# SwiGLU's first product by one level of Strassen's algorithm, in a hybrid gMLP and gated-linear-attention layer

## The chip, the cores and the metric

The kernel runs on one NeuronCore of a Trainium2 chip. A core has five engines with an instruction queue of their own: TensorE (PE; matmuls into PSUM, weights loaded by PEld), VectorE (DVE), ScalarE (ACT), GpSimd (POOL) and SyncE (SP), which here only issues DMAs. The metric is device microseconds of one launch; the fewer the better. A profiled execution gives the trace from which all rows are read.

## The reference

One layer of a diffusion trunk on 512 latent tokens of width 2048 with 256 context tokens. After the mixer comes the part that is changed:

```
x   = x + mod[2] * rms_norm(y @ w_out, g_post_mix)
h   = modulate(rms_norm(x, g_pre_ffn), mod[3], mod[4])      # 512 x 2048
a,b = split(h @ w_ffn_in, 2)                                # 2048 x 11264: a and b are 512 x 5632
f   = (silu(a) * b) @ w_ffn_out                             # 5632 x 2048
out = x + mod[5] * rms_norm(f, g_post_ffn)
mod = split(silu(c) @ w_mod + b_mod, 6)                     # w_mod 2048 x 12288
```

All inputs are float32.

## The kernel before

Every large product is made of float32r matmuls. An operand is split into two parts, a high one (a cast on ACT) and the rest (a subtraction on DVE), and `three` (L291) adds three products of the parts into one PSUM bank: high x high, high x low, low x high. So each weight tile of 128 rows and 512 columns costs one cast and one subtraction of 512 columns, and three matmuls for each stationary block of 128.

`stream` (L278) walks over the row tiles of a weight matrix: two row tiles per DMA of 512 KB on SP's queue, a split for each (four buffers for either part), then the caller's matmuls, then `pump` (L274), which emits some steps of background work: `bg` and `bgm` are lists of generators with a rate of steps per row tile. One of them is `mod_row` (L250): it sums 16 row tiles of w_mod times a per-partition scalar on DVE (L225, 1024 columns each, three load buffers, one accumulator), and adds up the partitions by a product with ones that is pinned in PE's order (`keep_in_program_order`). All other instructions are ordered by the planner of the framework: it takes, engine by engine, the first instruction in code order that is ready by its own model of durations, and the order so found is fixed in the program.

The stages that matter here, in order:

* Output projection (`project`, L984): four column blocks of w_out (tiles wo); the last is done for tokens 0 to 255 and 256 to 511 one after the other. Beside it run the modulation rows m20 and m21 (the gate of the mixer). `residual` (L994) and `make_h2` (L1013) of the first half of tokens run beside the last block's second half; `make_h2` transposes the normalised tokens on PE (tiles h2p), modulates on ACT and splits into h2h and h2l.
* SwiGLU: 11 groups of 512 hidden units. `ffn_in` (L1052) makes a and then b of a group, hidden-major: 16 row tiles x 4 blocks of 128 hidden units x 3 matmuls of 512 tokens (tiles f). The first group's a is done over the first 256 tokens and then over the others, since h2 of those comes later. `hidden` (L1062) applies SiLU, multiplies and splits (gh, gl). Every two groups (`chunks`) the second product follows (tiles fo): four column blocks x 8 row tiles x 4 token tiles x 3, added up in SBUF (facc). The modulation rows m50 and m51 run beside the chunks from the second on.
* The end: the last group's second product (fz), token tile by token tile, with norm, gate and residual behind each.

SBUF is shared out by hand: 44 slots of 512 columns (`slot`), 33 in a second pool (`fslot`), the stream's pool `stg`. PSUM has six banks for accumulation and two for all else (`bank`).

Of the kernel before, what the change touches and what calls it, by code (L numbers as in the profile page):

```python
# [18 lines left out]
P = 128  # L19
D = 2048  # L20
# [12 lines left out]
NF = 33  # L33
# [17 lines left out]
class Pump:  # L51
    """Background work, emitted in small steps between the steps of the weight streams; lanes take turns"""
# [39 lines left out]
def trunk_kernel(ctx, tc, cmat, cmask, x, c, ctxt, c_ctx, w_mod, b_mod, g_pre_mix, g_post_mix, g_pre_ffn,  # L92
# [7 lines left out]
    stg = ctx.enter_context(tc.tile_pool(name="stg", bufs=1))  # L100
# [13 lines left out]
    # ---- constants and small vectors  # L114
# [21 lines left out]
    def rstd(ss, n, scale, name, eng=None):  # L136
        """1 / sqrt(scale ss + eps): a first guess from the exponent's bits, then Newton steps"""
# [19 lines left out]
    def rstd_exp(ss, n, name):  # L157
        """the same for tokens' sums over four column blocks, from ScalarE's logarithm and exponential and a Newton step"""
# [24 lines left out]
    # ---- adaLN: w_mod columns in blocks, rows accumulated on VectorE, summed over partitions on TensorE  # L183
# [48 lines left out]
    def mod_ab(base, k0, nk, cvec, gv, A, B, name, tiles, pin=False, late=0):  # L232
        """shift and scale of nk channel tiles -> per-channel scalars A = g (1 + scale), B = shift"""
# [16 lines left out]
    def mod_row(base, cb, grow, dst, name):  # L250
        """1024 columns of a gate as rows (every partition), times the post-norm gain"""
        n = f"{name}{cb}"
        for acc in mod_acc(base + cb * 1024, 1024, 1, cx, n, mod_bg):
# [3 lines left out]
        for j in range(2):  # L257
# [5 lines left out]
            V.tensor_tensor(out=dst[b], in0=ps, in1=gb, op=ALU.mult)  # L263
            yield

    # ---- weights: streamed, split into two float32r parts
# [11 lines left out]
    def stream(w, c0, ncol, nk, name, k_first=0):  # L278
        """(k, [(hi, lo) per 512 columns]) for the 128-row tiles of w"""
# [11 lines left out]
    def three(o, a, b, start, stop, lhs_first=True):  # L291
        """o += a^T b from the parts of both; a is the stationary operand"""
# [7 lines left out]
    # ---- x: root mean square, transpose  # L300
# [6 lines left out]
    def squares(tok, ss, j):  # L307
        """a token tile's sums of squares"""
# [25 lines left out]
    def turn(o, tok, k, diag=None):  # L334
        """channel tile k, channel-major"""
# [22 lines left out]
    def gate_weights(name):  # L358
        """the 32 columns of w_in for the low-rank gates, all rows: both parts beside each other, per channel tile"""
# [11 lines left out]
    def low_rank(o, w, h, start, stop):  # L371
        """the gates' low-rank products: rows 0-31 with the high part of the weights, rows 32-63 with the low part"""
# [5 lines left out]
    def modulated(k):  # L378
        """channel tile k of x, normalised and modulated, in two float32r parts"""
# [17 lines left out]
    # ---- first products of x as the modulation arrives, in two halves of the channels: d, k and the last head of q;  # L397
    # the other heads of q
# [5 lines left out]
    def land(ps, dst, first, scale=1.0, rows=P):  # L404
        """a part of a sum over channels, or a further part onto it"""
# [5 lines left out]
    def mod_both(k0):  # L411
        """shift and scale of two channel tiles for x and for the context: products on TensorE, which waits for them"""
# [114 lines left out]
    # ---- context: normalised and transposed, modulated by its own adaLN  # L527
# [52 lines left out]
    # ---- spatial gating  # L580
# [65 lines left out]
    # ---- context: d, k, v  # L646
# [32 lines left out]
    # ---- gated linear attention  # L679
# [23 lines left out]
    def log_decay(dsrc, h, p, name):  # L703
        """log-sigmoid of the gates of head h, tokens of two chunks: [token, (chunk, direction, key)]"""
# [11 lines left out]
    def keyed(b, dr_, nch, kT, dst):  # L716
        """k exp(b_last - b)"""
# [52 lines left out]
    def gla_scores(h):  # L770
# [16 lines left out]
        # scores inside a chunk, both directions: S^T[j, i]  # L787
# [11 lines left out]
        def weigh(s):  # L799
            """k and q times the decays to the boundary of their half of a block of 2 s tokens"""  # L800
# [43 lines left out]
    def gla_states(h):  # L844
# [9 lines left out]
        # states  # L854
# [27 lines left out]
        # outputs, channel-major, over the head's k and q  # L882
# [32 lines left out]
    # ---- values of the attention, token-major  # L915
# [13 lines left out]
    # ---- output gate of the attention, and both halves split for the output projection  # L929
# [35 lines left out]
    # ---- output projection, residual, norm before the FFN  # L965
    fp = ctx.enter_context(tc.tile_pool(name="fp", bufs=1))
# [3 lines left out]

    gate = [slot(f"gm{b}") for b in range(4)]
# [9 lines left out]
    h2h = [None] * KT  # L981
    h2l = [None] * KT

    def project(cg, toks, name):  # L984
        accs = [bank(f"{name}{t}") for t in toks]
        for k, (wp,) in stream(w_out[0], cg * 512, 512, KT, name):
# [7 lines left out]
    def residual(t0):  # L994
        """of two token tiles: x1 = x + gate * norm(y), kept in DRAM; then x1 over its root mean square"""
# [17 lines left out]
    def make_h2(half):  # L1013
        o = half * 256
        for k0 in range(0, KT, 2):
            ps = bank(f"h2p{half}_{k0}", False)
            tmp = slot(f"h2f{half}_{k0}")
            for j in range(2):
                k = k0 + j
                c = slice(j * 256, (j + 1) * 256)  # L1020
                turn(ps[:, c], yo[half * 2:half * 2 + 2], k)
                S.activation(tmp[:, c], ps[:, c], AF.Identity, bias=fmodB[:, k:k + 1], scale=fmodA[:, k:k + 1])
                if half == 0:
                    h2h[k] = fslot(f"h2h{k}", F32R)
                    h2l[k] = slot(f"h2l{k}", F32R)
                V.tensor_copy(h2h[k][:, o:o + 256], tmp[:, c])
                V.tensor_tensor(out=h2l[k][:, o:o + 256], in0=tmp[:, c], in1=h2h[k][:, o:o + 256].bitcast(F32),
                                op=ALU.subtract)
# [7 lines left out]
    for half in range(2):  # L1036
# [4 lines left out]
        bg.add(make_h2(half))  # L1041

    # ---- SwiGLU, hidden units in chunks, the second product summed over chunks
    gate2 = [None] * 4

    def mods_ffn():
        for b in range(4):
            gate2[b] = slot(f"gf{b}")
        for b in range(2):
            yield from mod_row(5 * D, b, g_post_ffn, gate2, "m5")  # L1050

    def ffn_in(gi, part, cols=((0, 512),)):  # L1052
        accs = [bank(f"f{gi}{part}{b}") for b in range(4)]
        for c0, n in cols:
            if c0:
# [115 lines left out]
```

## Time and profile before

| | us |
|---|---|
| median of 3 runs | 2407.95 |
| lowest, highest | 2407.12, 2409.24 |
| span of the profiled execution | 2405.3 |
| PE, DVE, ACT busy in it | 2349.8, 1221.4, 863.7 |

The span runs from the first to the last instruction of the profiled execution; a launch's time holds in addition what lies before and behind, and the median of the runs is 2.65 us above the span. Busy time of PE is modelled from each matmul's start, and matmuls overlap in the pipeline, so the distance between starts tells the pace, not the duration.

### The profile page before, as it was taken

To read this page: it belongs to the slowest core of one execution; us is meant where nothing else is said; L and a number is where in the kernel's file an instruction comes from. 1 tells how busy PE (TensorE), PEld (TensorE's weight loads), DVE (VectorE), ACT (ScalarE), POOL (GpSimd) and SP (SyncE) were. 2 spreads that over 40 slices of the span, in tenths; PEclk is the share of its full clock that TensorE was granted. 3 is DMA by queue.
4 is the path that set the end of the run, shared out by engine and by line. 5 is a ranking of instruction groups with operands and counts; after the bars stand their busy time and mean duration, and the time that the engine had idled before them with its cause. 6 is when DMAs were issued, how large, how long until landed. Compare 5 with 4: busy or idle time off the path is not lost.

```text
span 2405.3 us, 28755 instructions
## 1 busy us (share of the span) xinstructions
PE 2349.8 (98%) x10930; PEld 1932.2 (80%) x10930; DVE 1221.4 (51%) x1958; ACT 863.7 (36%) x1595; POOL 15.3 (1%) x22
## 2 busy tenths in 40 slices
PE   7999998999999999999999999999999999999998
PEld 2778887788887787888888888888888888888886
DVE  3876587677878747533234344333323332323347
ACT  4453344554564237523332222232222322323223
POOL 0000000000000000000000000000000000000000
PEclk9999999999999999999999999999999999999999
DMA  9967788644446847533244444433333323333335
GB/s 333 330 195 261 252 280 269 205 140 132 132 148 211 300 160 224 166 96 97 97 149 140 140 132 149 140 121 99 97 97 97 96 97 97 97 97 97 97 104 184
DMA packets 197507, 381.91 MB, mean 159 GB/s; under 512 B 17349, under 2 KB 28829, under 8 KB 197369
## 3 DMA queue, kind: packets, MB, share of 16 engines
q1 hardware_dynamic: 192992, 373.88, 48.0%
q10 hardware_dynamic: 4376, 6.20, 0.8%
q8 instruction: 85, 1.39, 0.2%
q14 instruction: 54, 0.43, 0.1%
HBM read 367.44 MB, written 12.58 MB: 158 GB/s over the span
## 4 chain that ended last, share of the span: by engine, by line
PE 89%; DMA 4%; DVE 4%; ACT 2%; issue 1%; SPq 0%; ACTq 0%; DVEq 0%
PE f L112 40%; PE fo L112 17%; PE wo L112 6%; PE vv1a L112 2%; PE g0a L112 2%; PE v0a L112 2%; PE u1a L112 2%; PE cv L112 2%; PE k L112 2%; PE vv0a L112 2%; PE v1a L112 2%; PE q L112 1%; PE g1a L112 1%; PE u L112 1%; PE s L112 1%; PE o L112 1%
## 5 line engine op out<-in xcount | busy, mean ns | idle before, releaser
L112 PE MATMUL f<-h2h,f_0h 128*128 128x512 f32 (+1 forms) x1472 | 561.1, 381 | 5.3 <-ACT f_0h L270 5.3
L271 DVE TENSOR_TENSOR f_0l<-f_r,f_0h 128x512 fp32r<-128x512 f32 x368 | 253.8, 691 | 610.5 <-ACT f_0h L270 577.8
L112 PE MATMUL f<-h2l,f_0h 128*128 128x512 f32 (+1 forms) x1472 | 560.0, 381 | 0.0
L112 PE MATMUL f<-h2h,f_0l 128*128 128x512 f32 (+1 forms) x1472 | 559.4, 381 | 0.0
L270 ACT CAST f_0h<-f_r 128x512 fp32r<-128x512 f32 x368 | 229.1, 623 | 657.3 <-PE f L112 616.3
L112 PEld LDWEIGHTS f<-h2h,f_0h 128*128 128x128 f32 x1472 | 277.5, 189 | 58.5 <-ACT f_0h L270 5.5
L112 PEld LDWEIGHTS f<-h2l,f_0h 128*128 128x128 f32 x1472 | 277.5, 189 | 52.5 <-issue 0.5
L112 PEld LDWEIGHTS f<-h2h,f_0l 128*128 128x128 f32 x1472 | 276.9, 188 | 52.6 <-DVE f_0l L271 0.2
L112 PE MATMUL fo<-fo_0h,gh 128*128 128x512 f32 x640 | 249.8, 390 | 0.0
L112 PE MATMUL fo<-fo_0h,gl 128*128 128x512 f32 x640 | 249.0, 389 | 0.0
L112 PE MATMUL fo<-fo_0l,gh 128*128 128x512 f32 x640 | 249.0, 389 | 0.0
L271 DVE TENSOR_TENSOR fo_0l<-fo_r,fo_0h 128x512 fp32r<-128x512 f32 x160 | 110.5, 691 | 263.7 <-ACT fo_0h L270 253.6
L270 ACT CAST fo_0h<-fo_r 128x512 fp32r<-128x512 f32 x160 | 99.8, 624 | 306.6 <-PE fo L112 267.9
L112 PEld LDWEIGHTS fo<-fo_0l,gh 128*128 128x128 f32 x640 | 120.1, 188 | 25.4 <-DVE fc L1108 0.2
L112 PEld LDWEIGHTS fo<-fo_0h,gh 128*128 128x128 f32 x640 | 120.1, 188 | 25.4 <-issue 0.5
L112 PEld LDWEIGHTS fo<-fo_0h,gl 128*128 128x128 f32 x640 | 120.1, 188 | 24.8
L112 PE MATMUL wo<-wo_0l,yh 128*128 128x512 f32 x256 | 101.3, 396 | 2.1 <-DVE wo_0l L271 2.1
L112 PE MATMUL wo<-wo_0h,yh 128*128 128x512 f32 x256 | 102.0, 402 | 0.0
L112 PE MATMUL wo<-wo_0h,yl 128*128 128x512 f32 x256 | 101.6, 397 | 0.0
L112 PEld LDWEIGHTS wo<-wo_0l,yh 128*128 128x128 f32 x256 | 48.9, 191 | 13.5 <-DVE wo_0l L271 2.6
L112 PEld LDWEIGHTS wo<-wo_0h,yh 128*128 128x128 f32 x256 | 48.6, 190 | 10.8 <-issue 0.5
L112 PEld LDWEIGHTS wo<-wo_0h,yl 128*128 128x128 f32 x256 | 48.9, 191 | 10.2
(811 smaller groups left out, 3401.5 us busy)
## 6 DMA issues: line engine op xcount, KB each, us to landing
f_r<-in_w_ffn_in_dram SPq DMA_DIRECT2D x184, 512.0 KB
fo_r<-in_w_ffn_out_dram SPq DMA_DIRECT2D x80, 512.0 KB
mx4w<-in_w_mod_dram SPq DMA_DIRECT2D x16, 512.0 KB
mx8w<-in_w_mod_dram SPq DMA_DIRECT2D x16, 512.0 KB
mx12w<-in_w_mod_dram SPq DMA_DIRECT2D x16, 512.0 KB
mc4w<-in_w_mod_dram SPq DMA_DIRECT2D x16, 512.0 KB
mc8w<-in_w_mod_dram SPq DMA_DIRECT2D x16, 512.0 KB
mc12w<-in_w_mod_dram SPq DMA_DIRECT2D x16, 512.0 KB
```

What stands on the lines that cost most here:

```text
L112: return T.matmul(o, lhsT=l, rhs=r, start=start, stop=stop)
L270: S.copy(wh[:, :n], src)
L271: V.tensor_tensor(out=wl[:, :n], in0=src, in1=wh[:, :n].bitcast(F32), op=ALU.subtract)
```

## The change

The first product is one level of Strassen's algorithm in Winograd's form. h is cut in two halves of tokens (rows) and two of channels (columns): A11, A12 for tokens 0 to 255, A21, A22 for the others. A group's weights are cut in the two halves of channels and in the columns of a and of b: B11, B12, B21, B22. Seven products of 256 tokens x 1024 channels x 512 columns take the place of eight:

```
S1=A11 S2=A12 S4=A22 S5=A22-A21 S6=S5+A11 S7=A21-A11 S3=A12-S6     (once, in make_top and make_rest)
T1=B11 T2=B21 T5=B11+B12 T6=T5+B22 T4=T6+B21 T3=B22 T7=B12+B22     (per group, on DVE, in float32)
a of tokens 0-255 = P1+P2; the other three quarters from P1, P3 to P7 by sums of results
```

(the signs are those of the kernel's weight sums.) The S operands are split once and stay in SBUF (56 tiles); they are the stationary operand now and the weights move, so the results come token-major: each product has two PSUM banks, one per token tile. Of the weights, B11 to B22 are loaded 28 times 512 KB per group where it was 16, and each of the seven T is split by one cast and one subtraction of 1024 columns. After the results' sums, SiLU and product, 16 transposes per group turn the activations hidden-major, and they go to DRAM (`g_dr`). The second product starts when all groups are done, reads them back (`hidden`), splits them and runs in two chunks of 20 row tiles; the last four row tiles are the end, as before, with their weights loaded and split during the last column block.

Other parts: the pool `stg` is closed after the attention and a pool `st2` opened at the same side of SBUF, with four buffers X (the running T sum; loads and accumulators of the modulation rows too), four load buffers R, three of 1024 columns for either part. m50 and m51 are made beside the projection, behind m20 and m21, at a rate of 1.5 steps per row tile (1.2 before), and kept as rows in DRAM.

```diff
-NF = 33
+NF = 29
...
-    stg = ctx.enter_context(tc.tile_pool(name="stg", bufs=1))
+    stg_ctx = ExitStack()
+    stg = stg_ctx.enter_context(tc.tile_pool(name="stg", bufs=1, side="right"))
...
-    def mod_row(base, cb, grow, dst, name):
+    def mod_row(base, cb, grow, dst, name, tiles, keep=None):
...
+            o = gb if keep is not None else dst[b]
+            V.tensor_tensor(out=o, in0=ps, in1=gb, op=ALU.mult)
+            if keep is not None:
+                nc.scalar.dma_start(keep[b:b + 1, :], o[0:1, :])
...
+    stg_ctx.close()
+    fp = ctx.enter_context(tc.tile_pool(name="fp", bufs=1, reuse_waits="tile"))
+    st2 = ctx.enter_context(tc.tile_pool(name="st2", bufs=1, side="right", reuse_waits="tile"))
...
+    def parts(src, name):
...
+        wh = st2.tile([P, 1024], F32R, tag="wh", bufs=3, name=name + "h")
+        wl = st2.tile([P, 1024], F32R, tag="wl", bufs=3, name=name + "l")
+        S.copy(wh, src)
+        V.tensor_tensor(out=wl, in0=src, in1=wh.bitcast(F32), op=ALU.subtract)
+        return wh, wl
...
+    def stream2(w, c0, k_first, nk, name):
...
+        for k0 in range(0, nk, 2):
+            t = wide(w, (k_first + k0) * P, c0, raw2(f"{name}r{k0}"), name)
+            pair = parts(t, f"{name}{k0}")
+            for j in range(2):
+                yield k0 + j, cut(pair, j * 512, 512)
+                pump()
...
         for b in range(2):
-            yield from mod_row(2 * D, b, g_post_mix, gate, "m2")
+            yield from mod_row(2 * D, b, g_post_mix, gate, "m2", mod_late)
+        for b in range(2):
+            yield from mod_row(5 * D, b, g_post_ffn, None, "m5", mod_late, gate2_dr)
...
-    bgm.rate = 1.2
+    bgm.rate = 1.5
...
+    def make_top():
+        for i, p in ((0, 1), (1, 2)):
+            for q in range(NQ):
+                top[i][q] = h2_pair(0, i * KT // 2 + 2 * q)
+                s_parts(p, q, top[i][q], fslot)
+                yield
...
+    def make_rest():
+        for q in range(NQ):
+            a21 = h2_pair(1, 2 * q)
+            a22 = h2_pair(1, KT // 2 + 2 * q)
+            a11, a12 = top[0][q], top[1][q]
+            s_parts(4, q, a22, slot)
+            V.tensor_tensor(out=a22, in0=a22, in1=a21, op=ALU.subtract)
+            s_parts(5, q, a22, slot)
+            V.tensor_tensor(out=a22, in0=a22, in1=a11, op=ALU.add)
+            s_parts(6, q, a22, slot)
+            V.tensor_tensor(out=a21, in0=a21, in1=a11, op=ALU.subtract)
+            s_parts(7, q, a21, slot)
+            V.tensor_tensor(out=a12, in0=a12, in1=a22, op=ALU.subtract)
+            s_parts(3, q, a12, slot)
             yield
...
+    def product(p, q, accs, wp, nq):
+        hi, lo = SP[p][q]
+        for j in range(2):
+            for t in range(2):
+                c = slice(j * 256 + t * P, j * 256 + (t + 1) * P)
+                three(accs[t], (hi[:, c], lo[:, c]), cut(wp, j * 512, 512), q == 0 and j == 0, q == nq - 1 and j == 1)
...
+        ps = two(n + "p1")
+        for q in range(NQ):
+            X[q] = blk(0, 0, q, chain_tile(f"{n}X{q}"))
+            product(1, q, ps, parts(X[q], f"{n}a{q}"), NQ)
+            pump()
+        u = [fslot(f"{n}u{t}") for t in range(2)]
+        for t in range(2):
+            S.copy(u[t], ps[t])
+        ps = two(n + "p2")
...
+        if gi == 0:
+            bg.drain()
...
+        p5 = two(n + "p5")
+        for q in range(NQ):
+            r = blk(0, 1, q, raw2(f"{n}c{q}"))
+            V.tensor_tensor(out=X[q], in0=X[q], in1=r, op=ALU.add)
+            product(5, q, p5, parts(X[q], f"{n}c{q}"), NQ)
+        p6 = two(n + "p6")
...
+        vtt(u, u, p6, ALU.subtract)
+        u4 = [fslot(f"{n}w{t}") for t in range(2)]
+        vtt(u4, p5, u, ALU.add)
+        p4 = two(n + "p4")
...
+        vtt(u, p4, u, ALU.add)
...
+        p7, p3 = two(n + "p7"), two(n + "p3")
+        for q in range(NQ):
+            z = blk(1, 1, q, raw2(f"{n}z{q}"))
+            y = blk(0, 1, q, raw2(f"{n}y{q}"))
+            product(3, q, p3, parts(z, f"{n}z{q}"), NQ)
+            V.tensor_tensor(out=y, in0=y, in1=z, op=ALU.add)
+            product(7, q, p7, parts(y, f"{n}y{q}"), NQ)
+        vtt(u, u, p7, ALU.subtract)
+        for t in range(2):
+            S.activation(u[t], u[t], AF.Silu)
+        b2 = [fslot(f"{n}v{t}") for t in range(2)]
+        vtt(b2, p7, u4, ALU.subtract)
+        vtt(u4, p3, u4, ALU.subtract)
+        vtt(a1, a1, u4, ALU.mult)
+        vtt(u, u, b2, ALU.mult)
+        toks = a1 + u
+        for f in range(4):
+            ps = bank(f"{n}T{f}", False)
+            for t in range(NT):
+                T.transpose(ps[:, t * P:(t + 1) * P], toks[t][:, f * P:(f + 1) * P], ident)
+            gt = slot(f"{n}t{f}")
+            S.copy(gt, ps)
+            nc.scalar.dma_start(g_dr[gi * 4 + f], gt)
...
+    def hidden(k0, nk):
...
+        for k in range(k0, k0 + nk, 2):
+            r = raw2(f"gr{k}")
+            nc.sync.dma_start(r.rearrange("p (k c) -> p k c", k=2), g_dr[k:k + 2].rearrange("k p c -> p k c"))
...
+    for ci, (k1, nk) in enumerate(((0, 20), (20, 20))):
         gT = []
...
+            if ci and cg == 3:
+                bg.add(last_weights())
+                bg.rate = 0.5
```

(`vtt` does one DVE operation for each of two token tiles, `blk` loads a weight block of two row tiles, `two` takes two banks.)

## Rows read from the trace of the kernel before

**Rows 1.** The page: span, busy time per engine, GB/s per slice, costliest group.

```profile
span 2405.3 us, 28755 instructions
...
PE 2349.8 (98%) x10930; PEld 1932.2 (80%) x10930; DVE 1221.4 (51%) x1958; ACT 863.7 (36%) x1595; POOL 15.3 (1%) x22
...
GB/s 333 330 195 261 252 280 269 205 140 132 132 148 211 300 160 224 166 96 97 97 149 140 140 132 149 140 121 99 97 97 97 96 97 97 97 97 97 97 104 184
...
L112 PE MATMUL f<-h2h,f_0h 128*128 128x512 f32 (+1 forms) x1472 | 561.1, 381 | 5.3 <-ACT f_0h L270 5.3
...
```

**Rows 2.** Chain that ended last, SwiGLU: start us, length us, engine, tile, line, count.

```profile
...
979.36 151.26 PE f L112 x746
1130.62 87.04 PE fo L112 x384
1217.66 174.08 PE f L112 x768
...
```

**Rows 3.** Busy time by stretch, us; then TensorE clock, DMA share, GB/s.

```profile
...
802.00:842.00 40.00, 40.00 (x177) 32.83 (x176) 31.11 (x34) 7.80 (x13) 0.95 (x1) 1.00 0.88 303
...
940.70:979.40 38.70, 33.44 (x258) 32.48 (x258) 31.03 (x79) 29.02 (x66) 0.00 (x0) 0.91 0.68 212
...
2004.60:2265.70 261.10, 261.10 (x1153) 216.20 (x1152) 78.34 (x117) 71.73 (x118) 0.00 (x0) 1.00 0.33 97
2358.80:2405.30 46.50, 37.45 (x166) 30.67 (x164) 33.71 (x68) 13.58 (x40) 0.00 (x0) 0.94 0.44 162
...
```

**Rows 4.** The same chain at other places.

```profile
...
750.61 6.60 PE wo L112 x29
...
758.35 1.92 PE mf12ps L112 x16
...
927.44 0.44 PE h2p L339 x4
...
942.83 0.30 PE h2p L339 x2
943.12 0.83 PE f L112 x7
943.95 0.26 PE h2p L339 x2
...
967.48 0.97 PE h2p L339 x4
...
1413.51 0.86 PE m50ps L112 x2
...
2332.65 3.53 DMA fl<-in_w_ffn_out_dram
...
```

**Rows 5.** Groups by line, shapes apart: count | busy us, mean ns | idle before.

```profile
...
L339 PE MATMUL h2p<-mats,yo 128*128 128x128 f32 x64 | 12.8, 291 | 0.0
...
L271 DVE TENSOR_TENSOR f_0l<-f_r,f_0h 128x512 fp32r<-128x512 f32 x368 | 253.8, 691 | 610.5 <-ACT f_0h L270 577.8 <-PE f L112 32.5
...
L1069 DVE TENSOR_TENSOR fa<-fa,f 128x512 f32<-128x512 f32 x44 | 28.1, 680 | 0.0
...
L826 DVE TENSOR_TENSOR lv<-lv,kq 128x1024 f32<-128x1024 f32 x20 | 24.4, 1219 | 3.8 <-ACT lv L825 3.8
...
L1066 ACT ACTIVATE fa<-f 128x512 f32<-128x512 f32 x44 | 26.0, 600 | 4.5 <-PE f L112 2.8
...
L825 ACT ACTIVATE lv<-lv 128x1024 f32<-128x1024 f32 x20 | 21.0, 1055 | 13.5 <-DVE lv L824 13.4
...
L1022 ACT ACTIVATE h2f<-h2p,fmodB,fmodA 128x256 f32<-128x256 f32 x32 | 17.2, 573 | 2.4 <-PE h2p L339 2.4
...
```

**Rows 6.** Modulation rows' sums (ns min/median/max, first and last start), and a wait.

```profile
...
L225 DVE SCALAR_TENSOR_TENSOR m20acc<-m20w,cpair,m20acc x16: 1271/1284/1287, 765.4 to 799.2; 128x1024 f32<-128x1024 f32 x16
...
L225 DVE SCALAR_TENSOR_TENSOR m21acc<-m21w,cpair,m21acc x16: 1276/1284/1286, 807.9 to 840.4; 128x1024 f32<-128x1024 f32 x16
...
PE m20ps L112 <- DVE m20acc L225: 3.0, 1, 3.0
...
```

More of the change, by code (lines that the diff above doesn't have):

```diff
@@ L1011, in residual @@
             V.tensor_scalar(out=yo[t0 + 1][b], in0=yo[t0 + 1][b], scalar1=r[:, 1:2], scalar2=None, op0=ALU.mult)
[L1013 to L1028, printed above, removed]
+    NQ = KT // 4
@@ new lines, in trunk_kernel, with s_parts, h2_pair @@
+    SP = {p: [None] * NQ for p in range(1, 8)}
+    def s_parts(p, q, src, new):
+        hi, lo = new(f"S{p}h{q}", F32R), new(f"S{p}l{q}", F32R)
+        S.copy(hi, src)
+        V.tensor_tensor(out=lo, in0=src, in1=hi.bitcast(F32), op=ALU.subtract)
+        SP[p][q] = (hi, lo)
+    def h2_pair(half, k0):
+        ps = bank(f"h2p{half}_{k0}", False)
+        tmp = slot(f"h2f{half}_{k0}")
+        for j in range(2):
+            k = k0 + j
+            c = slice(j * 256, (j + 1) * 256)
+            turn(ps[:, c], yo[half * 2:half * 2 + 2], k)
+            S.activation(tmp[:, c], ps[:, c], AF.Identity, bias=fmodB[:, k:k + 1], scale=fmodA[:, k:k + 1])
+        return tmp
@@ new lines, in trunk_kernel @@
+    top = [[None] * NQ for _ in range(2)]
+    def make_top():
[18 more added lines that the diff above has]
+            s_parts(3, q, a12, slot)
@@ L1040, in trunk_kernel @@
         bg.add(residual(2 * half))
[L1041 to L1055, printed above, removed]
-                bg.drain()
-            for k, (wp,) in stream(w_ffn_in[0], part * HID + gi * 512, 512, KT, f"f{gi}{part}_{c0}_"):
-                for b in range(4):
-                    three(accs[b][:, c0:c0 + n], cut(wp, b * P, P), cut((h2h[k], h2l[k]), c0, n), k == 0, k == KT - 1)
-        return accs
@@ L1079, in two_parts @@
-    def two_parts(b):
-        pool_tile = mod_bg[0 if b < 3 else 1]
-        p = pool_tile(f"gx{b}").bitcast(F32R)
-        return p[:, :512], p[:, 512:]
-    bgm.rate = 0.25
-    facc = [[None] * 4 for _ in range(NT)]
-    chunks = ((0, 1), (2, 3), (4, 5), (6, 7), (8, 9))
-    for ci, groups in enumerate(chunks):
-        if ci == 1:
-            bgm.add(mods_ffn())
-        gT = []
-        for gi in groups:
-            gT += hidden(gi)
-        if ci == len(chunks) - 1:
-            bgm.drain()
-            gT_last = hidden(10, [two_parts(b) for b in range(4)])
-            exp_tables()
+        bg.add(make_rest() if half else make_top())
@@ new lines, in product, with two, each, vtt @@
+    def product(p, q, accs, wp, nq):
+        hi, lo = SP[p][q]
+        for j in range(2):
+            for t in range(2):
+                c = slice(j * 256 + t * P, j * 256 + (t + 1) * P)
+                three(accs[t], (hi[:, c], lo[:, c]), cut(wp, j * 512, 512), q == 0 and j == 0, q == nq - 1 and j == 1)
+    def two(name):
+        return [bank(f"{name}{t}") for t in range(2)]
+    def each(ts, ps, f, name=None):
+        for i in range(2):
+            f(ts[i], ps[i])
+    def vtt(out, a, b, op):
+        for i in range(2):
+            V.tensor_tensor(out=out[i], in0=a[i], in1=b[i], op=op)
@@ new lines, in trunk_kernel @@
+    for gi in range(HID // 512):
+        ffn_group(gi)
+    facc = [[None] * 4 for _ in range(NT)]
+    def hidden(k0, nk):
+        for k in range(k0, k0 + nk, 2):
+            r = raw2(f"gr{k}")
+            nc.sync.dma_start(r.rearrange("p (k c) -> p k c", k=2), g_dr[k:k + 2].rearrange("k p c -> p k c"))
+            for j in range(2):
+                hi, lo = slot(f"gh{k + j}", F32R), slot(f"gl{k + j}", F32R)
+                S.copy(hi, r[:, j * 512:(j + 1) * 512])
+                V.tensor_tensor(out=lo, in0=r[:, j * 512:(j + 1) * 512], in1=hi.bitcast(F32), op=ALU.subtract)
+                yield (hi, lo)
@@ new lines, in trunk_kernel, with last_weights @@
+    LAST = 4
+    wl_ = []
+    def last_weights():
+        for cg in range(4):
+            for k0 in (0, 2):
+                r = wide(w_ffn_out[0], (HID // P - LAST + k0) * P, cg * 512, raw2(f"fl{cg}{k0}"), "fl")
+                for j in range(2):
+                    c = r[:, j * 512:(j + 1) * 512]
+                    new = slot if cg > 1 else fslot
+                    hi, lo = fslot(f"flh{cg}{k0 + j}", F32R) if cg < 1 else slot(f"flh{cg}{k0 + j}", F32R), \
+                        slot(f"fll{cg}{k0 + j}", F32R)
+                    S.copy(hi, c)
+                    V.tensor_tensor(out=lo, in0=c, in1=hi.bitcast(F32), op=ALU.subtract)
+                    wl_.append((hi, lo))
+                yield
```

86 lines of the change are left out of this document (48 added, 38 removed).

## Prediction

> **What bounds the kernel now.** I began with the page's busy shares [rows 1]: TensorE (PE) is busy for 98% of a span of 2405.3 us, VectorE (DVE) for half of it, ScalarE (ACT) for a third. Such a kernel gets faster only by fewer or cheaper matmuls, as long as nothing new makes PE wait. The chain that ended last shows where this holds without a gap [rows 2]: in the SwiGLU it is an unbroken line of matmuls. Two groups of the first product, 768 matmuls of 512 columns, take 174.08 us, so one matmul every 226.7 ns and 87.04 us for a group of 384; the second product has the same pace (384 in 87.04). The page's group of them says 381 ns for one [rows 1]; that is a pipelined duration, so I cost by the spacing. [...]
>
> **What is removed.** Before, a group has 2 parts x 16 row tiles x 4 blocks x 3 = 384 matmuls. After, it has 7 products x 4 pairs x 2 x 2 token tiles x 3 = 336 of the same width, in the same pattern of a stationary operand used twice, then once: 48 x 0.2267 = 10.88 us less per group.
>
> **What is added on PE.** 16 transposes per group. Four transposes of the same shape (h2p) stand in a row in 0.44 us [rows 4], so 0.11 each, 1.76 us per group: 76.16 + 1.76 = 77.92 us against 87.04. [...] Over the ten later groups the two together are 10 x (77.92 - 87.04) = **-91.2 us**.
>
> **What is added on DVE and ACT.** Per group: 28 splits of 1024 columns, 16 sums of weight blocks of 1024, 18 sums of results of 512. A two-operand 1024 op took 1219 ns, a 512 split 691, a 512 op with a PSUM operand 680 [rows 5]; the 1024 split has no row, I take 1.23 (between 1.22 and twice 0.69, nearer the row of its own width). So 28 x 1.23 + 16 x 1.22 + 18 x 0.68 = 66.2 us of DVE against 77.9 of PE: it fits, but 85% full. ACT: 28 casts at about 1.055 (the 1024 exponential's) + 10 small ones at 0.60 = 35.5 us [rows 5]. DMA: 28 loads of 0.52 MB in 78 us = 188 GB/s, under the 303 seen; one load landed in 3.5 us [rows 4], and four buffers turn over quicker than the 2.72 us that PE needs per pair.
>
> Inside a group the tight stretch is products 5, 6 and 4: per pair a sum and a split, 2.45 us of DVE against 2.72 of PE, and 2.7 us of result sums at two ends. But DVE has 50% spare in products 1 and 2, and the next block's sum can run ahead there, as the previous pair's tile is already split. Three split buffers keep PE up to 5.4 us ahead. I cost this stretch at nothing; its price without the lead is the third rival.
>
> **The end of a group** is a chain: product 7's last matmul, then ten DVE ops (10 x 0.68 = 6.9 us, SiLU on ACT beside them), then the transposes. Behind the transposes stand, in code order, the next group's matmuls. The planner need not keep code order: the transposes that make h2 are written in fours, and come out in twos with seven matmuls between them [rows 4]. So the next group's first two pairs (5.4 us) can go ahead, as many as the split buffers allow beside the one in use. The third pair's split stands behind the ten ops on DVE, at 8.1 us. PE then idles 8.1 - 5.4 - about 1.2 of transposes = 1.5 us. With fixed orders that were planned on modelled times I take twice that, 3 us: 11 x 3 = **+33** (bounds 0.5 and 8.5 per group).
>
> **The first group.** Today two groups and the end of h2 take 189.9 us, from 940.7 [rows 3] to 1130.6 [rows 2]; minus 87.04: 102.9, with one wait of 5.3 us [rows 1] and a clock of 0.91 in the first 38.7 us [rows 3], because the residual of tokens 256 to 511 is late. Its transposes start at 967.5 [rows 4], 26.8 us after the stage's start. After, products 1 and 2 (96 matmuls, 21.8 us) cover this about as today's pass over half the columns does (192 of half the width). New is what follows: for each of four quarters 5 splits and 4 sums of 512 on DVE, 5 x 0.69 + 4 x 0.68 = 6.2, in all 24.7 us, before product 5 can end: 26.8 + 2.3 (four evictions of 573 ns [rows 5]) + 24.7 + 2.7 = 56.5 us against 36.1 without stall (144 matmuls, 32 transposes). So 77.9 + 3.5 + 20.4 = 101.8, and 2 for what queues behind the loads of x: 103.8, **+0.9** (bounds -12, with splits made while the residual waits, and +15, with ACT held as now).
>
> **The projection stage** now carries four modulation rows instead of two, 64 loads of 0.52 MB. A row's 16 sums took 35.1 us (765.4 to 799.2 and one more of 1.28), and the next row began 42.5 after the first [rows 6], as there is one accumulator. The products that close a row are pinned in PE's order: PE stood 3.0 us for m20 [rows 6] with the projection's matmuls behind it. The accumulator now comes from the same four buffers as the loads, so I take 36 us a row: from 760 to 904. PE reaches the last pinned product, by code behind the third column block, at 757.2 + 48 x 2.72 + 1.9 (mf12 [rows 4]) + 6.9 (16 row products at 0.43 [rows 4]) = 896.6, where 757.2 is the end of the projection's first matmuls [rows 4]. So **+8** (0 if a row takes 33; 38 at 42.5). The m5 products leave the SwiGLU as they come in here, which cancels. [...]
>
> The new buffers lie over the closed pool's. Of the projection's first matmuls 29 (6.6 us [rows 4]) run while mf12's row is still summed; a split buffer that lies on those loads' memory has to wait: **+4** (0 to 11).
>
> **The rest.** The second product keeps its 1920 matmuls, in two chunks for five. Its activations come from DRAM: per two row tiles 1.23 + 2 x 0.69 = 2.6 us of DVE under 5.4 of PE; without that cover 0.7 a row tile, 14 us in a chunk. 64 result ops become 32, off the path. The end goes by the same chain as now (PE 37.45 of 46.5 us [rows 3]): 0 (-3 to +3).
>
> **Sum**: -91.2 + 33 + 0.9 + 8 + 4 = -45.3. On the profiled span 2360.0; the median of the runs is 2.65 above the span, so **2363 us**.
>
> **Rivals.** (1) *Everything hides*: 0.5 us per boundary, projection and buffers 0: -91.2 + 5.5 + 0.9 = -84.8, **2323**. For it: PE has hardly a gap from 979 us on. Against: DVE's share there more than doubles. (2) *The modulation rows hold the projection*: 38 + 11 instead of 12: **2400**. For it: that stretch ran at 0.88 of DMA. Against: of m21's 33.8 us only 16 x 1.28 = 20.5 were sums, so a buffer more can help. (3) *DVE becomes the bound*: if in products 5, 6 and 4 each pair pays sum, cast and split one after the other, 1.22 + 1.06 + 1.23 = 3.5 instead of 2.72, it is 9.4 us per group and 103 in all; with half of it **2415**, slower. It turns the change into a loss from 4.1 us per group. For it: 85% load on an engine that waits for another in the middle of each pair. Against: sums can fill the wait for the cast. (4) *The transposes hold PE's queue* for the ten ops and the copies between their banks, 8.5 us a group instead of 3: +60, **2424**, slower, deciding above 7.1 us. For it: m20's 3.0 us. [...] Against: it was pinned, and the transposes are not.
>
> **Numbers.** Under 0.2% (4.8 us) a measurement of this kernel tells nothing from no change. My forecast 0.50 (own range 2340 to 2387), rival 1 0.15, rival 2 0.13, rival 3 0.12, rival 4 0.10. Faster: 0.50 + 0.15 + 0.09 of (2) + 0.03 of (3) = 0.77; slower 0.02 + 0.08 + 0.09 = 0.19; same 0.04. Range 2316 to 2412: it leaves out a third of (1), most of (4) and half of (3).
>
> **What would show it.** 3696 matmuls of the first product at 227 ns; a later group near 81 us. At each group's end two pairs of the next product ahead of the transposes, and PE idle 1 to 3 us; if 7, rival 4. In products 5, 6, 4 PE waiting for DVE's split means rival 3. m51's products near 905 us with PE standing; if not, rival 1. The first group near 104 us with its waits inside product 5. The prediction is wrong if the loads at 188 GB/s land late, which no term prices, or if the spacing of matmuls changes.

## The result: slower by 0.65%, and the profile after

The changed kernel took **2424.89 us** (median of 4 runs, 2421.92 to 2426.19) against 2407.53 of the kernel before beside it: a ratio of **1.0065**, 95% interval 1.005 to 1.0079. The forecast was 2363 us, its range 2316 to 2412; the result lies outside it and on the other side of no change. The profiled execution has a span of 2424.4 us, 19.1 more than [rows 1].

The page of the kernel after, the same lines as in [rows 1]:

```profile
span 2424.4 us, 27761 instructions
...
PE 2319.1 (96%) x10386; PEld 1851.2 (76%) x10386; DVE 1596.3 (66%) x2040; ACT 987.7 (41%) x1509; POOL 15.3 (1%) x22
...
GB/s 322 334 195 251 239 282 245 239 131 134 127 105 177 314 299 310 226 131 191 185 188 219 189 190 184 219 195 188 180 218 193 171 139 96 96 172 101 102 139 156
...
```

PE has 544 instructions less than before and is busy for 30.7 us less, yet the span is longer: PE stands for 105 us of it, before for 56. DVE went from 51% to 66%. In the slices from 788 to 970 us (the 14th to the 16th), DMA moved 314, 299 and 310 GB/s where [rows 1] has 300, 160 and 224.

The stages come from the first and last starts of a few tiles' matmuls in the view of a tile's instructions (duration ns min/median/max, first and last start us). After:

```profile
...
L113 PE MATMUL mf12ps<-mats,mf12acc x16: 343/352/352, 769.4 to 772.6; 128*128 128x1 f32 x16
...
L113 PE MATMUL f0p<-f0a0h,S1h x4: 392/397/479, 990.2 to 993.2; 128*128 128x512 f32 x4
...
L113 PE MATMUL f1p<-f1a0h,S1h x4: 390/394/404, 1107.0 to 1109.1; 128*128 128x512 f32 x4
...
L113 PE MATMUL fo<-fo_0h,gh x64: 390/393/796, 1923.6 to 2321.1; 128*128 128x512 f32 x64
...
L113 PE MATMUL fz<-flh,gh x64: 387/389/399, 2372.0 to 2414.9; 128*128 128x512 f32 x64
...
```

By these, with before's from the same view and [rows 2]; the last column is experiment 3 below:

| stage, us | forecast change | before | after | after, tiles shifted |
|---|---|---|---|---|
| up to the last mf12 product | 0 | 760.0 | 772.6 | 759.4 |
| output projection, to the first SwiGLU matmul | +12 (8 and 4) | 180.4 | 217.6 | 219.2 |
| first group | +0.9 | 103.2 | 116.8 | 116.3 |
| ten later groups (before: ten of 87.04) | -58.2 (-91.2 and 33 at the ends) | 870.4 | 816.6 | 804.3 |
| second product (before with its m5 products) | 0 | 438.6 | 448.4 | 437.3 |
| last hidden units and the end | 0 | 52.7 | 52.4 | 52.4 |
| span | -45.3 | 2405.3 | 2424.4 | 2388.9 |

Two rows cannot come from Strassen: the stages ahead of the change, whose code is the same, end 12.6 us late, and the second product, with its 1920 matmuls as before, takes 10 us more though the m5 products have left it. The chain of waits of the kernel after (start us, length us, engine, tile, line, count) says how:

```profile
...
1438.09 71.35 PE f5p L113 x307
...
1923.62 448.52 PE fo L113 x1920
2372.15 43.58 PE fz L113 x192
```

These are stretches without a wait. 307 matmuls in 71.35 us are one every 232.4 ns and 1920 in 448.52 one every 233.6, where [rows 2] has 226.7; but the last 192 keep 227.0. The granted clock was 1.00 in the middle of both. So TensorE's clock is not it: each matmul takes 6 to 7 ns longer, nearly everywhere, and the last stage differs in something. Its weights lie in tiles of s2 and fp. All other weights lie in stg or its successor st2, the pools that the change moved to the right side of SBUF. In the built program, every tile of stg started 864 bytes past a multiple of 1024 before, like those of s2 and fp; afterwards those of stg and st2 start at 992.

### The profile page after: what moved, and what is told of

It reads as the page before. It is cut to its first block, busy times and chain, and to the rows that moved or that the text cites. A ratio compares the mean times of both kernels' runs of the same rounds, so it can differ in the third digit from the quotient of the medians.

```text
span 2424.4 us, 27761 instructions
## 1 busy us (share of the span) xinstructions
PE 2319.1 (96%) x10386; PEld 1851.2 (76%) x10386; DVE 1596.3 (66%) x2040; ACT 987.7 (41%) x1509; POOL 15.3 (1%) x22
## 4 chain that ended last, share of the span: by engine, by line
PE 81%; DMA 8%; DVE 6%; ACT 3%; issue 1%; SPq 0%; ACTq 0%; DVEq 0%
PE fo L113 19%; PE f7p L113 3%; PE f4p L113 3%; PE f9p L113 3%; PE f5p L113 3%; PE f1p L113 3%; PE f6p L113 3%; PE f3p L113 3%; PE f2p L113 3%; PE f10p L113 3%; PE f8p L113 2%; PE f0p L113 2%; PE v0a L113 2%; PE u1a L113 2%; PE g0a L113 2%; PE cv L113 2%
## 5 line engine op out<-in xcount | busy, mean ns | idle before, releaser
L1221 DVE TENSOR_TENSOR gl<-gr,gh 128x512 fp32r<-128x512 f32 x44 | 28.4, 687 | 24.2 <-ACT gh L1220 24.2
L1220 ACT CAST gh<-gr 128x512 fp32r<-128x512 f32 x44 | 25.1, 618 | 28.1 <-DMA gr<-g_dr 20.9
L113 PE MATMUL fo<-fo_0h,gh 128*128 128x512 f32 x64 | 26.4, 412 | 1.7 <-ACT gh L1220 1.7
L113 PE MATMUL vv0a<-vv_0h,hxh 128*128 128x512 f32 x64 | 27.7, 433 | 0.0
L113 PE MATMUL vv1a<-vv_0h,hxh 128*128 128x512 f32 x64 | 27.1, 424 | 0.0
L113 PE MATMUL g1a<-hxh,g_0h 128*128 128x512 f32 x64 | 26.6, 415 | 0.3 <-ACT g_0h L274 0.3
L113 PE MATMUL g0a<-hxh,g_0h 128*128 128x512 f32 x64 | 26.9, 420 | 0.0
L113 PE MATMUL v1a<-v_0h,hxh 128*128 128x512 f32 x64 | 26.7, 417 | 0.0
L113 PEld LDWEIGHTS s<-lv 128*128 128x128 f32 x192 | 24.9, 191 | 2.0 <-issue 0.5
L113 PE MATMUL fo<-fo_0l,gh 128*128 128x512 f32 x64 | 26.0, 407 | 0.0
```

Source lines behind the costliest of these rows:

```text
L113: return T.matmul(o, lhsT=l, rhs=r, start=start, stop=stop)
L1220: S.copy(hi, r[:, j * 512:(j + 1) * 512])
L1221: V.tensor_tensor(out=lo, in0=r[:, j * 512:(j + 1) * 512], in1=hi.bitcast(F32), op=ALU.subtract)
```

## The experiments

All are timed against the kernel before on the same chip, but for the fourth, which is a single run.

**1. Only the side of SBUF.** The kernel before, with nothing of the change but this:

```diff
-    stg = ctx.enter_context(tc.tile_pool(name="stg", bufs=1))
+    stg = ctx.enter_context(tc.tile_pool(name="stg", bufs=1, side="right"))
```

> The kernel before with one edit: the pool of the raw, high and low weights (stg) is opened on the right side of SBUF, as the changed kernel opens it; every tile of it then starts 992 bytes past a multiple of 1024 instead of 864, while the other operands' tiles (s2, fp) stay at 864. Nothing of Strassen is in it. Theory A (the matmuls of the changed kernel are spaced by 232 to 234 ns instead of 226.7 because of where their operands' tiles start): spacing of u1a, f and fo 232 to 234 ns, and with some 12 us up to the end of mf12ps as in the changed kernel and 1420 us / 226.7 ns x 6 to 7 ns = 38 to 44 us from the first SwiGLU matmul on, a time of 2450 to 2465 us. Theory B (it is the load on VectorE, ScalarE and DMA, or the order of instructions, of the changed kernel): spacing 226.7 ns and the time of before, 2408 us.

2455.44 us, ratio 1.0198 (1.0185 to 1.0212): theory A. Its chain:

```profile
...
1234.99 179.20 PE f L112 x768
...
2403.16 44.82 PE fz L112 x192
```

768 matmuls of the first product take 179.20 us, 233.3 ns each, against 174.08 in [rows 2]. Here fz is slow too: its stationary operands are tiles of stg in this kernel.

**2. The same, moved by 128 bytes**, so that stg's tiles on the right side start at 864 again:

```diff
+    padp = ctx.enter_context(tc.tile_pool(name="padp", bufs=1, side="right"))
+    pad = padp.tile([P, 32], F32, name="pad")
+    nc.gpsimd.memset(pad, 0.0)
     stg = ctx.enter_context(tc.tile_pool(name="stg", bufs=1, side="right"))
```

> The kernel before with stg on the right side and a 128-byte tile between it and the end of SBUF, so that all its tiles start 864 bytes past a multiple of 1024 again, like those of s2 and fp. Theory A1 (the start of the tiles modulo some power of two counts, absolutely or one operand against the other): spacing 226.7 ns, time of before, 2408 us, within 5 us. Theory A2 (the upper end of SBUF is slower to read, or the distance between the operands counts): spacing 232 to 234 ns, 2450 to 2465 us, as with stg on the right alone. Theory B: 2408 us, as before.

2409.59 us, ratio 1.0007 (0.9997 to 1.0017). The side costs nothing; the start of the tiles cost 46 us.

**3. The changed kernel with the same three lines** ahead of its stg, which moves stg and st2.

> The changed kernel with one edit: a 128-byte tile at the end of SBUF, so that every tile of stg and st2 starts at 864 instead of 992 past a multiple of 1024. Theory A1: spacing back at 226.7 ns in u1a, f and fo, mf12ps ends near 760, ten later groups take some 796 instead of 816.5 us, the second product 435 instead of 448.5 us: 2425 less 12, 21 and 13 is 2378 us, of which the modulation rows of the projection may take some back, since they wait for loads (2372 to 2395 us). Theory A2 and theory B: 2425 us, no change.

2392.58 us, ratio **0.9934** (0.9918 to 0.995): 32 us less than the changed kernel took, and faster than before. The table's last column is its profile: the first stage and the second product are back. The expectation had 47 us; the medians differ by 32 and the two profiled executions by 35.5: 13 in the first stage, 12 instead of 21 in the ten groups, 11 in the second product, and nothing in the projection (219.2), which waits for something else. Why the groups gave only 12 is not shown.

**4. The pace by itself**: series of 36 products with the stationary and the moving operand at eight starts each, and nothing else of the computation.

> Matmuls alone (the rest of the computation is left out: no output of the reference is made): series of 36 products of 128x128 by 512 columns in float32r, for eight starts of the stationary and eight of the moving operand modulo 1024 (A 864, B 896, C 928, D 992, E 0, F 128, G 256, H 352), tile qXY for stationary X and moving Y; hXY with the moving operand at the upper end of SBUF; wXY with VectorE and ScalarE at work. Theory A1, relative: qAA, qDD 226.7 ns, qAD and qDA 232 to 234 ns. Theory A1, absolute: all with a D slow, qDD too. Theory A2: q all 226.7, h slow. Theory B: q and h all 226.7 ns, w slower.

The timeline of PE (start us, modelled length, tile, count); the spacing is the difference of two starts over 36:

```profile
...
39.46 8.32 PE L46 MATMUL qAA<-mv,st 128*128 128x512 f32 x36
47.62 8.57 PE L46 MATMUL qAB<-mv,st 128*128 128x512 f32 x36
...
64.28 8.53 PE L46 MATMUL qAD<-mv,st 128*128 128x512 f32 x36
72.64 8.59 PE L46 MATMUL qAE<-mv,st 128*128 128x512 f32 x36
...
147.84 8.35 PE L46 MATMUL qBF<-mv,st 128*128 128x512 f32 x36
156.02 8.55 PE L46 MATMUL qBG<-mv,st 128*128 128x512 f32 x36
...
264.81 8.34 PE L46 MATMUL qDD<-mv,st 128*128 128x512 f32 x36
272.99 8.57 PE L46 MATMUL qDE<-mv,st 128*128 128x512 f32 x36
...
573.50 8.32 PE L46 MATMUL hAA<-mh,st 128*128 128x512 f32 x36
581.65 8.55 PE L46 MATMUL hAD<-mh,st 128*128 128x512 f32 x36
590.05 8.56 PE L46 MATMUL hDA<-mh,st 128*128 128x512 f32 x36
...
606.62 8.33 PE L46 MATMUL wAA<-mv,st 128*128 128x512 f32 x36
614.79 8.55 PE L46 MATMUL wAD<-mv,st 128*128 128x512 f32 x36
623.18 8.56 PE L46 MATMUL wDA<-mv,st 128*128 128x512 f32 x36
...
```

qAA takes 47.62 - 39.46 = 8.16 us, 226.7 ns each. qDD is fast too (8.18, 227.2) and qAD slow (8.36, 232.2), so it is not an address as such but one operand against the other; and A and D differ by 128 bytes, so being equal modulo 128 is not enough. qBF is fast (8.18, 227.2): its starts, 896 and 128, differ by 768, so they need not be equal modulo 512. Of the 64 pairs, exactly the 14 whose starts are equal modulo 256 bytes have 226.7 to 227.2 ns; the other 50 have 229.2 to 234.4. At the upper end of SBUF (hAA 8.15, hAD 8.40) and beside VectorE and ScalarE (wAA 8.17, wAD 8.39) it is the same. So theory A1 in its relative form; A2 and B fall.

**5. The m5 rows out of the projection**, in the kernel of experiment 3:

```diff
             yield from mod_row(2 * D, b, g_post_mix, gate, "m2", mod_late)
+
+    def mods_ffn():
         for b in range(2):
             yield from mod_row(5 * D, b, g_post_ffn, None, "m5", mod_late, gate2_dr)
...
         ffn_group(gi)
+    bgm.add(mods_ffn())
+    bgm.rate = 0.5
...
     bg.drain()
+    bgm.drain()
```

> The changed kernel with the tiles of stg and st2 moved by 128 bytes, and its two m5 modulation rows taken out of the output projection and put beside the second product (rate 0.5, the same tiles, bgm drained ahead of the last hidden units). Theory C (the projection is held by transfers: with four rows it moves 67 instead of 50 MB at some 300 GB/s): the stretch from the end of mf12ps to the first SwiGLU matmul falls from 219 us to 180 to 186 us, the second product gains under 5 us: 2392.6 - 36 to 40 + 0 to 5 = 2353 to 2362 us. Rival D (the projection's 38 us come from the wider weight tiles and their split, or from the pinned products of the rows, not from the bytes): 2385 to 2395 us. Rival E (the rows only move their cost, to the second product): 2385 to 2395 us with the projection near 183 us and the second product some 30 us longer.

2379.71 us, ratio 0.9887 (0.987 to 0.9904): 13 us better than experiment 3 (11 by the two ratios), not 31 to 40. Theory C holds for half of the stage's loss. The projection fell from 219.2 to 199.8 us, half the way. The second product rose by 9.3: 3.4 for the m5 products and 5.7 at its head, where its first loads now waited for the last group's store (g_dr<-f10t in the chain). The expectation also counted w_out twice: with rows of 8.4 MB and five column blocks of 4.2 MB it is 54.5 MB against 37.7, not 67 against 50.

**6. The converse, one part of the change alone**: in the kernel before, the m5 rows join the projection.

```diff
...
         for b in range(2):
             yield from mod_row(2 * D, b, g_post_mix, gate, "m2")
+        for b in range(2):
+            yield from mod_row(5 * D, b, g_post_ffn, None, "m5", gate2_dr)
...
-    bgm.rate = 1.2
+    bgm.rate = 1.5
...
```

> The kernel before with one part of the change alone: its two m5 modulation rows leave SwiGLU's second group and join the output projection (rate 1.5), their result through DRAM. Theory C: the projection stage goes from 180 us to 215 to 225 us, SwiGLU gives back 3 us: 2407 + 32 to 42 = 2439 to 2449 us. Rival D (transfers hide, the changed kernel's projection is slow for its other edits): 2404 to 2412 us.

2435.75 us, ratio 1.0117 (1.0099 to 1.0134); the projection takes 210.6 us, 30 more. Theory C, a little under its range. What the rows do in the changed kernel stands in the chain ahead of the last pinned product:

```profile
...
934.10 4.03 DMA m51w<-in_w_mod_dram
...
938.23 1.29 DVE m51acc L226
...
939.57 1.98 PE m51ps L113 x4
941.55 21.70 PE wo L113 x93
...
```

A load of w_mod, its sum, then m51ps at 939.57, with 93 matmuls of the projection behind it. But PE hardly stands there. What it waited for, in the views of the tiles wo and m51ps (us, times):

```profile
...
  ACT wo00h L989: 7.8, 1
  DVE yo L1029: 7.2, 1
...
  DVE m51acc L226: 2.5, 1
...
```

The 2.5 us are the pinned product. The 7.2 us, up to 889.6, are the third column block's first product, which waits until DVE has taken earlier results (yo) out of PSUM; in DVE's order these stand behind sums of m50, and those wait for their loads. The 7.8 us are the first weight tile. The whole stage, from mf12 to the first SwiGLU matmul, in windows of the kernel before, the changed one, experiment 3 and experiment 5 (length, then busy us of PE, weight loads, DVE, ACT, POOL; clock, DMA share, GB/s):

```profile
...
760.20:940.40 180.20, 175.10 (x757) 141.52 (x757) 118.99 (x174) 71.39 (x141) 2.86 (x3) 0.98 0.68 228
...
772.90:990.20 217.30, 194.55 (x803) 151.65 (x803) 156.95 (x161) 69.27 (x108) 3.82 (x4) 0.95 0.91 306
...
759.70:978.60 218.90, 194.66 (x804) 153.25 (x804) 157.51 (x161) 69.55 (x108) 3.82 (x4) 0.93 0.90 305
...
760.30:959.80 199.50, 186.80 (x796) 150.71 (x797) 116.32 (x125) 69.24 (x108) 1.90 (x2) 0.95 0.72 243
...
```

With four rows the loads run at 305 to 306 GB/s for the whole stage, and it takes the same time at either pace of the matmuls. PE stands for 23 us instead of 5, and the granted clock is lower on average (0.95 and 0.93 against 0.98). Behind the longest waits of the changed kernel it was 0.60 (780.7 to 790 us, behind the 7.8 us, and 890 to 895, behind the 7.2), and 1.00 from 790.2 to 795. Behind the 2.5 us it was 1.00, and m51ps's four products have a median length of 592 ns; in experiment 3, behind a wait of 3.9 us, they have 1061, and the clock from 920 to 940 us is 0.83. So a part of the loss can be matmuls at a lower clock; it was not separated.

**7. Where the new tiles lie.** Half of the projection's 38.8 us was left. In the kernel of experiment 5, the raw tiles of st2 are put over stg's, which come free early, and X over the attention's:

```diff
+    G.memset(chain_tile("first")[:, :8], 0.0)
     mod_late = (chain_tile, chain_tile, load_behind)
```

> The kernel with the m5 rows late, and the tiles of st2 in another order: the four X tiles lowest (over the attention's pool gl), the four R tiles next (over stg's raw, high and low tiles, which are free some 25 us earlier). Theory F (the projection starts late because the new pools lie over gl and over the mf12 rows' tiles: the loads of w_out wait for kq and mf12acc, so that nothing fills PE between 725 and 760, where the kernel before ran 42 matmuls of wo, and PE stands until 767): the R loads land ahead of 757, the first wo matmul comes near 763, no wo0r piece in the chain; 8 to 10 us less than with the m5 rows late alone, 2368 to 2373 us. Rival G (the stall is the queue behind the mf12w loads, not the tiles' places): within 2 us of it.

2382.56 us, ratio 0.9885 (0.9866 to 0.9904): no change, theory F not confirmed. The first w_out load now went out at 749.69 us, but the first wo matmul again came at 768.3. It waited 6.9 us for ACT's cast of its weights (767.2), which in ACT's order stood behind the casts of the last activations (until 765.9). The subtraction on DVE came at 770.0, behind m20's first sum, which had waited until 768.8 for its tile and its bias; and 12.7 us of the SP queue went on the wait for the new X tile.

**8. Closing the pool, alone.** The kernel of experiment 2 with one edit (stg stands in an ExitStack now):

```diff
...
-    fp = ctx.enter_context(tc.tile_pool(name="fp", bufs=1))
+    stg_ctx.close()
+    fp = ctx.enter_context(tc.tile_pool(name="fp", bufs=1, reuse_waits="tile"))
+    stg = ctx.enter_context(tc.tile_pool(name="st2", bufs=1, side="right", reuse_waits="tile"))
+    mod_bg = mod_pool(stg, 3, 1, load_behind)
```

> The kernel before with stg on the right side and moved by 128 bytes, as measured at 2409.6 us, and one more edit: stg is closed ahead of the output projection and a pool of the same tiles is opened in its place, waits kept by tile, as the changed kernel does it. Nothing else of the change. Theory F (what a new pool's first transfer waits for is what lay in its place; here only the weights of the stage before, in tiles of the same places): the w_out loads start as early as before, some 40 wo matmuls run ahead of 760 again, 2407 to 2413 us. Rival J (closing a pool costs by itself, whatever lay there, because the new pool waits for the last use of the old one, the mf12 rows at 757): the first wo matmul near 767, 12 to 20 us slower, 2421 to 2430 us.

2420.85 us, ratio 1.0054 (1.0037 to 1.007), against 1.0007 with stg left open: **11 us** for closing a pool and opening the same one in the same place: in the built program its raw, high, low and modulation tiles lie where stg's lay. The tile-wise waits (`reuse_waits`) of st2 and fp came with it and were not tried apart. Rival J, a little under its range. The SP queue's timeline, first with stg open (experiment 2), then closed:

```profile
...
698.85 0.37 SPq L194 DMA_DIRECT2D wo0r<-in_w_out_dram  x1
...
705.80 0.38 SPq L194 DMA_DIRECT2D wo0r<-in_w_out_dram  x1
...
720.08 0.37 SPq L194 DMA_DIRECT2D wo0r<-in_w_out_dram  x1
721.90 24.72 SPq L202 DMA_DIRECT2D mf12w<-in_w_mod_dram  x8
...
```

```profile
...
714.40 37.01 SPq L203 DMA_DIRECT2D mf12w<-in_w_mod_dram  x13
751.47 0.46 SPq L195 DMA_DIRECT2D wo0r<-in_w_out_dram  x1
...
```

With the pool open, three loads of w_out go out ahead of the mf12 loads, which trickle in as their sums allow; closed, the first stands behind all 13 of them. The chain of experiment 8 shows the gap:

```profile
...
749.12 8.59 issue
757.70 3.56 PE mf12ps L116 x16
...
764.75 0.53 ACT wo_0h L274
...
765.32 0.79 PE wo L116
...
```

PE has nothing to do ahead of mf12ps, which waits for its sum; with the pool open (experiment 2) 41 matmuls of the projection ran between 725 and 760 us. The loads are not all of it: the casts of the same weights changed places in ACT's order too. With the pool open and closed (duration ns, first and last start us):

```profile
...
L273 ACT CAST wo_0h<-wo0r x16: 602/625/642, 722.4 to 788.7; 128x512 fp32r<-128x512 f32 x16
...
L274 ACT CAST wo_0h<-wo0r x16: 612/618/625, 764.7 to 803.7; 128x512 fp32r<-128x512 f32 x16
...
```

Closed, the first follows at once on a cast of the last activations, which had waited for DVE, so no load was waited for there. Theory F, by which the place alone counts, falls.

**9. The same, with the first raw tile over the attention's pool** (the new pool 4096 bytes larger at its upper end).

> As the run with stg closed and opened again, the new pool being 4096 bytes larger at its upper end, so that its first raw tile lies over the last kilobytes of the attention's pool gl and the others are moved by one raw tile. Theory F: the first load of w_out waits for the last instruction of the attention (kq, near 760) and the SP queue behind it, so that no wo matmul runs ahead of 760: 10 to 19 us slower than with the pool reopened in its own place. Rival J: the same time as that run, within 3 us.

2425.25 us, ratio 1.0075 (1.0057 to 1.0092): 4 us more than experiment 8, but the intervals overlap. By these times the closing is the greater part and the place at most the smaller.

**10. The first group.** In the kernel of experiment 7, the next group's products 1 and 2 fill the time in which the first waits for its operands, and the m5 rows start one column group later:

```diff
...
         if gi == 0:
+            ahead[1] = first_two(1, False)
             bg.drain()
...
-    bgm.add(mods_ffn())
...
+            if not ci and cg == 1:
+                bgm.add(mods_ffn())
```

> As the run before, and two more edits: products 1 and 2 of group 1 are put ahead of group 0's product 5 (X of group 1 loaded again for its product 5), and the m5 rows begin with the second column group of the second product. Theory H (the first group takes 115 instead of 79 us because its products 5, 6 and 4 wait for S4 to S7, which VectorE and ScalarE make between 965 and 1040): 21.8 us of other matmuls lie in that time now, groups 0 and 1 together take 170 to 178 us instead of 194, and the second product starts without its wait for g_dr (5.7 us): 20 to 28 us less than the run before. Rival I (PE's time there is lost to the casts of the weights in ScalarE's queue, which the new products lengthen as well): groups 0 and 1 stay at 190 us or more, 3 to 8 us less.

2367.47 us, ratio 0.9826 (0.9809 to 0.9842), 15 us less. The two groups went from 196.3 to 186.3 us and the second product from 445.9 to 440.7: between H and I. The stretch in question, windows of experiment 5 and then of experiment 11, which has the same order (busy us of PE, weight loads, DVE, ACT, POOL; clock, DMA share, GB/s):

```profile
...
1000.00:1040.00 40.00, 29.91 (x109) 20.50 (x110) 33.67 (x44) 22.12 (x35) 0.00 (x0) 0.88 0.36 111
...
```

```profile
...
1000.00:1040.00 40.00, 32.17 (x136) 24.24 (x135) 39.00 (x48) 25.06 (x40) 0.00 (x0) 0.93 0.57 171
...
```

The filler brought its own splits: DVE is now busy for 39.00 of 40 us, and PE gained 2.3. With the filler, DVE is the bound of this stretch; without it DVE has 6 us left there.

**11. The order of tiles of experiment 7 taken back.**

> The fastest kernel so far (group 1's first two products ahead of group 0's fifth, m5 rows late) with the X tiles highest in st2 again, as the changed kernel has them. The order of the tiles moved the time by 2.9 us the wrong way in one comparison, within the scatter of the two; if that was real, 2362 to 2366 us, if not, 2365 to 2370 us.

**2364.85 us**, ratio **0.9826** (0.9805 to 0.9848), the same as experiment 10: the order does nothing. It is the fastest version found, 42 us under the kernel before.

## Why the prediction was wrong

**The step that failed is one that the prediction named as its last condition and priced at nothing: the spacing of matmuls.** Every term of PE was worked out at 226.7 ns. The pool's new side changed the start of its tiles by 128 bytes modulo 256, and the pace of nearly all matmuls with it, from 226.7 to 232.4 and 233.6 ns. Shown by experiments 1 to 4; it is worth 32 us in the changed kernel (2424.89 against 2392.58) and turns its sign: with it mended the change is a gain of 0.66%.

Even so the gain is 15 us (experiment 3) and not 45, for two more terms failed.

**The projection term was mis-sized, and its mechanism was only half right**: 8 and 4 forecast, 38.8 measured at the old pace. Rival 2 held in that the modulation rows hold the stage, and its upper bound of 38 for them was not passed: they cost 19 us (experiment 5) to 30 (experiment 6). But the prediction had PE stand at the pinned products. m51's came at 939.6, not 905, and PE stood 2.5 us for them; the time went on the stage's loads at 305 GB/s, on sums that wait for them in DVE's order and, by a share that was not separated, on the lower clock (0.95 against 0.98 on average). The mistake was to take 36 us a row from a stretch with two rows, where rows of four, loads of the projection and loads of the first group shared the stage's 305 to 306 GB/s. The sum had slips besides: 904 - 896.6 is 7.4, at 42.5 us a row it is 33.4 and not 38, and the 896.6 counts the 37 matmuls that had run by 757.2 once more. The 4 for tiles that lie over others had the wrong mechanism: the main cost is that the projection's first loads and casts, and so its first matmuls, fell behind the mf12 row in the orders of SP and ACT. It measured 11 us alone, 15 with the tile over gl (bounds 0 to 11). Why the closed pool sends them behind was not shown. With 19 and 15 for the two parts, some 4 us of the 38.8 stay open; with the 30 of experiment 6, measured in the other kernel, the parts would be more than the whole.

**The first group** cost 13 us instead of 0.9, near the upper bound of 15. As forecast, its waits lie ahead of product 5: of the 21 us that PE stood in the changed kernel's first group, 9.3 went on casts of S5, one of that product's operands. With the filler of experiment 10, DVE was busy for 39.00 us of the 40 from 1000 to 1040. The clock was 0.90 in the group (0.97 before), which no term priced.

**The ends of the groups** were over-priced. With the starts mended the ten groups take 80.4 us each, the last one's full end included, and nine of them follow each other by 79.3 (1094.9 to 1808.6): 77.92 and 1.4 more, about the 1.5 that the prediction worked out and then doubled. The last group, which has no next one to cover its end, takes 90.6; so the ten ends cost 25 us together, where 33 was forecast for eleven. The kernel after shows the way that it described:

```profile
...
1429.02 4.43 PE f5p L113 x19
1433.45 0.22 PE f4T L1202 x2
1433.67 0.47 PE f5p L113 x2
1434.14 0.22 PE f4T L1202 x2
...
1435.35 1.05 ACT f5b0h L989
...
1436.94 1.15 PE f4T L1202 x8
...
```

19 matmuls of the next product go ahead of the transposes (f4T), those come in twos, and PE waits for 1.6 us at a cast. The last eight take 1.15 us, 0.14 each. So rival 4 is refuted. Rival 3 is too, outside the first group: from 1107 to 1905 us PE is busy for 795.5 of 798 us with DVE at 617, and in experiment 3 for 791.1 of 795 from 1095 on. By this the prediction's other last condition, loads that land late, cost next to nothing there. (In the second product the result sums on DVE went from 64 to 16, not to 32; they are off the path, as it said.)

So: forecast -45.3 on the span; projection 26.8 worse, first group 12.2 worse, later groups 7.9 better, the second product 1.3 better (its m5 products gone), the first and last stages 0.9 better. That gives -16.4, the span of experiment 3 against [rows 1], and the pace adds 35.5 by the profiled executions.

## What to carry to other kernels

Before a pool is moved, look at where its tiles start against the operands that TensorE pairs them with, and compare the spacing of matmuls in stages that the change doesn't touch: a uniform few per cent there can be an address and not the algorithm (here 233.6 ns against 226.7 in the second product). A pool that is closed and opened again can put the next stage's first loads and casts later in their queues (in experiment 8 the loads behind the 13 of mf12, the first cast at 764.7 us instead of 722.4), and the matmuls that filled gaps there are lost: 41 of them, in a kernel that took 11 us more. Background loads have to be priced with all the bytes of their stage, not by the time that one of them took among fewer; and where PE stands, look at the granted clock of the matmuls behind the wait (0.60 in the changed kernel behind 7.2 us, 1.00 behind 2.5).

## What the runs showed of the hardware

In experiment 4, the spacing of 512-column float32r products that change the stationary tile each time went by the start of the stationary against the moving operand, modulo 256 bytes: 226.7 to 227.2 ns in the 14 pairs with equal starts and 229.2 to 234.4 in the 50 others, at 1.00 granted clock. With VectorE and ScalarE at work, a series of 36 took 8.17 us (wAA, equal) and 8.39 (wAD, unequal); without, 8.16 (qAA) and 8.36 (qAD). Eight starts of either operand were run, with this shape and type alone. What makes the 50 slow is not shown.
